# Branch b's last eight outputs through ScalarE, written orders around them, and w_out's first products in two pairs

## The chip, the cores and the metric

The kernel runs on one core of one Trainium2 chip. The metric is the time of one execution in device microseconds (us); a version is told by the median of several executions.

## What is computed

One residual block over a sequence of 1024 positions of width 1024, in float32. Two branches are mixed, gated and projected, and a feed-forward network follows:

```python
def mixer(h, w_in, b_f, conv_w, w_branch, w_out):
    proj = jnp.einsum("bsd,dn->bsn", h, w_in)
    q, k, v, f_logit, g_b, g_c, hc, gate_conv, gate_attn = jnp.split(proj, _SPLITS, axis=-1)
    ya = g_b * causal_depthwise_conv(g_c * hc, conv_w)
    ...
    yb = forgetting_attention(q, k, v, logf)          # 8 heads of 64, 512 wide
    ya_d = jnp.einsum("bsc,cd->bsd", ya, w_branch[0])
    yb_d = jnp.einsum("bsc,cd->bsd", yb, w_branch[1])
    merged = jax.nn.sigmoid(gate_conv) * ya_d + jax.nn.sigmoid(gate_attn) * yb_d
    return jnp.einsum("bsd,de->bse", merged, w_out)
...
x = x + rmsnorm(mixer(rmsnorm(x, ...)), ...)
x = x + rmsnorm(swiglu(rmsnorm(x, ...), w_gate_up, w_down), ...)
```

The lines of this case are the `yb_d` product with its gate and sum (here "branch b") and the first part of the product with `w_out`.

## The kernel before

**How products are formed.** Each float32 operand is cut into a high part (a ScalarE copy into a reduced format, `hi`) and a low part (a VectorE subtraction, `lo`); `split` does both. A product is three matmuls, high by high, high by low, low by high (`mm3`), each of 128 x 128 by 128 x 512. Large products are done by a Strassen scheme of seven block products named by their left operands: A11, A12, A22, S1, S2, S3, S4, with right operands B11, B21, B22, T1 to T4. Left operands of `w_branch` and right operands of `w_out` were prepared earlier and stored (`wb_dram`, `wo_dram`); here they are only loaded.

**Orders.** The framework orders each engine's instructions itself by its own estimate of due times. `strict[0]` names engines whose instructions, from there on, keep the order in which the program text issues them; the wrapper `InOrder` (lines 65 to 80; line 77 issues every instruction, so all profile rows carry L77) marks each such instruction. Instructions issued while their engine is not named may still be moved among the others. Before the change the stretch from line 1546 to 1597 has `("tensor", "sync")`: matmuls and the loads on SyncE's (SP's) queue keep the written order, VectorE and ScalarE do not.

**Branch b (lines 1505 to 1593).** The result `um` has eight tiles d of 128 rows by two halves of columns, n1 and n2. For u = 0 to 3 the scheme gives four outputs, tiles 2u and 2u + 1 in n1 and n2. Eight PSUM banks are held, `pbanks[u]` and `vbanks[u]`. A first loop (1569) does S2, S4, S3 for each u: ScalarE copies the sum in `pbanks[u]` to `u_s[u]`, VectorE adds `vbanks[u]` to it, ScalarE puts the saved product `p_s[u]` back into `vbanks[u]`, and after S3 VectorE adds `pbanks[u]` to `v_s[u]`. `merge` then multiplies an output by its gate and adds it to `um`, two VectorE operations. `u_s` and `v_s` are eight slices of one tile, `temps`, in the place "x2". A second loop (1587) does A22 into `pbanks[u]` and A12 into `vbanks[u]`, in the order `turn_ = (3, 0, 1, 2)`; both are merged by VectorE straight from PSUM.

**Gates.** `gate(d, ns)` (1496) issues a load of a gate tile on SP's queue; the gate of tile 7 was stored before its sigmoid, so for d = 7 it also issues a Sigmoid on ScalarE on what was loaded. Gates of n1 use four `sg` tiles; those of turns u = 2 and 3 are loaded at the end of turns 0 and 1 of the first loop, when a tile comes free. Gates of n2 for u = 3 and 0 use other free tiles; those for u = 1 and 2 follow in `sg`.

**w_out (from 1598).** `um` is cut by rows of the sequence into four pairs of blocks. `first_ops(i)` cuts the first block of pair i into hi and lo, `sums(i)` forms its Strassen sums (on GpSimd for i = 0, on VectorE otherwise). `first(i)` is A11 by B11 into a bank `p1`, copied by ScalarE; `second(i)` is A12 by B21 into a bank `q`, added by VectorE. The loop at 1744 does first(0), first(1), second(0), first(2), second(1), first(3), second(2), second(3). Then `p_s2(0)` is the first product with T2, whose tile `x_tile(2)` has the place "x2"; S1, S3, S4 and A22 follow for each pair, with T1, T3, B22 and T4.

Of the kernel before, what the change touches and what calls it, by code (L numbers as in the profile page):

```python
# [47 lines left out]
def block_kernel(  # L48
# [16 lines left out]
    n1, n2 = slice(0, NC), slice(NC, S)  # L65
    engines = ("tensor", "vector", "scalar", "gpsimd", "sync")
    strict = [()]
# [42 lines left out]
    def add(o, a, b):  # L110
        nc.vector.tensor_tensor(o, a, b, op=ALU.add)
# [4 lines left out]
    def mul(o, a, b):  # L116
        nc.vector.tensor_tensor(o, a, b, op=ALU.mult)
# [11 lines left out]
    def copy(o, a):  # L129
        nc.scalar.activation(o, a, AF.Copy)  # L130

    def split(hi, lo, src):

        copy(hi, src)
        sub(lo, src, f32(hi))
# [399 lines left out]
    def flat(t):  # L535
        return t.rearrange("p a b -> p (a b)")
# [4 lines left out]
    def wtile(tag, bufs, dt=F32, shape=(P, KT, P)):  # L541
        return wpool.tile(list(shape), dt, tag=tag, name=tag, bufs=bufs)

    def raw_t():
        return wtile("raw", 3)

    def hi_t():
        return wtile("hi", 4, F32R)

    def lo_t():  # L550
        return wtile("lo", 3, F32R)

    def s4_t():
        return wtile("s4", 1, F32, (P, 4, P))
# [57 lines left out]
    def bank(psp, name):  # L612
        return psp.tile([P, NC], F32, tag="mm", name=name)

    def prod(ps, w, b, first):
        (ah, al), (bh, bl) = w, b
        kw = {} if first else dict(skip_group_check=True)
        for k in range(4):
            mm3(
                ps,  # L620
                (ah[:, k, :], al[:, k, :]),
                (bh[:, k, :], bl[:, k, :]),
                first and k == 0,
                k == 3,
                **kw,
            )
# [529 lines left out]
    def sg_tile():  # L1156
        return tp_.tile([P, NC], F32, tag="sg", name="sg", bufs=4)
# [281 lines left out]
    def x_tile(n, p=None):  # L1439
        if n == 3:  # L1440
            p, tag = yb_pool, "yb"
        else:
            p, tag = p or wx, f"x{n}"
        return p.tile([P, 2, 4, NC], F32R, tag=tag, name=f"x{n}", bufs=1)
# [6 lines left out]
    def load_wo(o, k):  # L1451
        nc.sync.dma_start(f32(wo[o][:, :, k, :]), wo_dram[o, k])

    PAIRS = ST // 2
    firsts, s3 = [None] * PAIRS, [None] * PAIRS

    def blocks(i):

        a, b = (slice(t * P, (t + 1) * P) for t in (2 * i, 2 * i + 1))
        return um[:, LO, a], um[:, UP, a], um[:, LO, b], um[:, UP, b]  # L1460

    def first_ops(i, th, tl):
        a = slice(2 * i * P, (2 * i + 1) * P)
        if i:
            split(th, tl, um[:, :, a])
            firsts[i] = dict(A11=(th[:, LO], tl[:, LO]), A12=(th[:, UP], tl[:, UP]))
        else:
            firsts[i] = {}
            for o, src, h, l in zip(("A11", "A12"), blocks(i), th, tl):
                split(h, l, src)  # L1470
                firsts[i][o] = h, l

    def kept_halves(t):
        return t[:, n1], t[:, n2]

    def minus(i, o, a, b, op=ALU.subtract):
        e = nc.vector if i else nc.gpsimd
        e.tensor_tensor(o, a, b, op=op)

    def sums(i, t):  # L1480

        a11, a12, a21, a22 = blocks(i)
        s3[i] = t
        minus(i, t, a11, a21)
        minus(i, a21, a21, a22, ALU.add)
        minus(i, a11, a21, a11)
        minus(i, a12, a12, a11)
# [6 lines left out]
    v_s, u_s = ([temps[:, 4 * i + u, :] for u in range(4)] for i in range(2))  # L1494

    def gate(d, ns, sg=None):
        sg = sg_tile() if sg is None else sg
        nc.sync.dma_start(sg, sg_dram[d][1, :, ns])
        if d == KT - 1:
            nc.scalar.activation(sg, sg, AF.Sigmoid)  # L1500
        return sg

    def prod_b(ps, o, u, b, first):
        (wh, wl), (bh, bl) = wb[o], tb[b]
        kw = {} if first else dict(skip_group_check=True)
        for k in range(2):
            m = 4 * k + u
            mm3(
                ps, (wh[:, m, :], wl[:, m, :]), (bh[:, k, :], bl[:, k, :]),
                first and k == 0, k == 1, **kw,  # L1510
            )

    def merge(d, ns, t, c, sg):
        mul(t, c, sg)
        add(um[:, d, ns], um[:, d, ns], t)
# [18 lines left out]
    pbanks = [psm.tile([P, NC], F32, tag="mm", name="pbp") for _ in range(4)]  # L1534
# [23 lines left out]
    vbanks = [psm.tile([P, NC], F32, tag="mm", name="pbv") for _ in range(4)]  # L1558
    for u in range(4):
# [4 lines left out]
    late = [  # L1564
        x for t in (wtile("raw", 3), wtile("sx", 1)) for x in kept_halves(flat(t))
    ]
    turn_ = (3, 0, 1, 2)
    late = [gate(2 * u + 1 - x, n2, late.pop(0)) for u in turn_[:2] for x in range(2)]
    for u in range(4):
        sg2, sg1 = early[2 * u : 2 * u + 2]  # L1570
        prod_b(pbanks[u], S2, u, T2, False)
# [9 lines left out]
            early += [gate(2 * u + 4 + x, n1) for x in range(2)]  # L1581
    first_ops(0, [s4h_t(), s4h_t()], [s4l_t(), s4l_t()])
    sums(0, s4_t())
    late += [gate(2 * u + 1 - x, n2) for u in turn_[2:] for x in range(2)]
    for u in range(4):
        load_wo(B21, u)
    for u in turn_:
        sg1, sg2 = late.pop(0), late.pop(0)
        prod_b(pbanks[u], A22, u, T4, False)
        merge(2 * u + 1, n2, sg1, pbanks[u], sg1)  # L1590
        prod_b(vbanks[u], A12, u, B21, False)
        merge(2 * u, n2, sg2, vbanks[u], sg2)
    for n, o in ((3, T1), (2, T2)):
        wo[o] = x_tile(n)
        for k in range(4):
# [27 lines left out]
    def square(src, acc):  # L1623
        junk = ep.tile([P, NC], F32, tag="junk", name="junk")
        nc.scalar.activation(junk, src, AF.Square, accum_out=acc)

    sx = wtile("sx", 1)
    for i in range(1, PAIRS):
        first_ops(i, hi_t(), lo_t())
        sums(i, ep.tile([P, 4, P], F32, name="s3") if i == 3 else sx[:, 4 * i - 4 : 4 * i])  # L1630

    def load_xt(st):
        xt = ep.tile([P, D], F32, name="xt") if st % 3 == 2 else z_tile("xt")
        nc.gpsimd.dma_start(xt, x2d[st * P : (st + 1) * P, :])
        return xt
# [7 lines left out]
    def first(i):  # L1643
        b1s[i] = pk.tile([P, NC], F32, tag="p1", name="p1")
        prod(b1s[i], firsts[i]["A11"], wob[B11], True)
        t = raw_t() if i < 3 else ep.tile([P, KT, P], F32, name="keep")
        keeps.append(flat(t))
        copy(keeps[i][:, n2], b1s[i])

    def second(i):  # L1650
        q = bank(psm, "q")
        prod(q, firsts[i]["A12"], wob[B21], True)
        add(keeps[i][:, n1], keeps[i][:, n2], q)
        square(keeps[i][:, n1], qas[i][:, 0:1])
# [86 lines left out]
                pinned(turns, "tensor")  # L1741
                ahead(lambda: copy(um[:, 4 * q : 4 * q + 4, ss], tp))

    for step in (0, 1, 2, 3):
        first(step)
        if step:
            second(step - 1)
    second(PAIRS - 1)
    wo[B22] = x_tile(0)
    wob[B22] = both(wo[B22])  # L1750
    for k in range(4):
# [145 lines left out]
    for f in range(NF):  # L1897
# [15 lines left out]
        for g, u, ns in ((g1, u1_, n1), (g2, u2, n2)):  # L1913
            sg = sgs[:, ns]
# [268 lines left out]
```

## Time and profile before

| | |
|---|---|
| median of 3 executions | 1319.69 us (1318.58 to 1319.75) |
| the profiled execution | 1319.07 us, of which the span 1317.3 us |
| granted TensorE clock, mean | 0.999 |
| TensorE busy | 1302.7 us, 99% of the span |
| VectorE busy | 981.4 us, 75% |
| ScalarE busy | 568.4 us, 43% |
| GpSimd busy | 153.6 us, 12% |

Times in rows of the profile are counted from the first instruction of the span; PE is TensorE, DVE VectorE, ACT ScalarE, POOL GpSimd, SPq the queue on which SP issues loads. A row names the tiles as written from read (`temps<-temps,pbp`), then the shapes, a count, and in brackets how long the engine was idle before and what ended that. `pbp` is `pbanks`, `pbv` is `vbanks`, `p` and `q` are the banks of first and second, `x<-wo_dram` are loads of w_out's operands. Branch b's two loops lie at about 564 to 593 us, w_out's eight first products at about 594 to 618 us.

### The profile page before, as it was taken

How to read it: one execution, taken by the hardware profiler on the slowest of the kernel's cores; microseconds unless marked ns; L12 is line 12 of the kernel's file. 1: busy time of each engine (PE TensorE's matmuls, PEld its weight loads, DVE VectorE, ACT ScalarE, POOL GpSimd, SP SyncE). 2: the span in 40 equal slices, each digit the busy share in tenths (PEclk: the TensorE clock that was granted, in tenths of full speed). 3: DMA queues.
4: the chain of work that ended last, by engine and by line, in shares of the span. 5: the costliest groups of instructions: out<-in, count | busy, mean ns of one | idle time of the engine just before them, and what ended most of it. 6: DMA issues, size and time to landing. Idle time of an engine off the chain costs nothing.

```text
span 1317.3 us, 18043 instructions
## 1 busy us (share of the span) xinstructions
PE 1302.7 (99%) x6686; PEld 1084.8 (82%) x6686; DVE 981.4 (75%) x1525; ACT 568.4 (43%) x902; POOL 153.6 (12%) x287
## 2 busy tenths in 40 slices
PE   9999999999999999999999999999999999999997
PEld 8988888888888888877888888888888888888886
DVE  6975978776656877587798789986766776676685
ACT  6642432254455866433676522222232234444452
POOL 0001100021112212020011021211101110000000
PEclk9999999999999999999999999999999999999999
DMA  6347755677846444489266555553323338866541
GB/s 221 110 119 224 196 162 146 168 250 214 240 144 200 162 140 150 154 312 403 81 228 203 160 165 172 184 176 104 104 81 120 105 119 290 311 242 195 156 166 64
DMA packets 207240, 235.13 MB, mean 178 GB/s; under 512 B 12064, under 2 KB 150368, under 8 KB 207152
## 3 DMA queue, kind: packets, MB, share of 16 engines
q1 hardware_dynamic: 159424, 157.13, 38.1%
q0 software_dynamic: 18544, 62.17, 12.8%
q10 hardware_dynamic: 29184, 14.68, 4.5%
q8 instruction: 52, 0.85, 0.3%
q14 instruction: 36, 0.29, 0.1%
HBM read 161.79 MB, written 72.16 MB: 178 GB/s over the span
## 4 chain that ended last, share of the span: by engine, by line
PE 72%; issue 17%; DMA 4%; POOL 2%; DVE 2%; ACT 1%; SPq 0%; POOLq 0%; DVEq 0%; ACTq 0%
PE b L77 37%; PE pd L77 16%; PE pba L77 3%; PE pv L77 3%; PE tps L77 3%; PE po L77 3%; PE p L77 2%; PE sp L77 2%; PE ma L77 1%; PE q L77 1%; PE tp L77 1%; POOL wb_dram L77 1%; DMA x<-wo_dram 1%; DMA raw<-in_w_gate_up_dram 1%; DMA sg<-sg_dram 1%
## 5 line engine op out<-in xcount | busy, mean ns | idle before, releaser
L77 PE MATMUL b<-x,hi 128*128 128x512 f32 x1088 | 335.3, 389 | 0.0
L77 PEld LDWEIGHTS b<-x,hi 128*128 128x128 f32 x1088 | 204.1, 188 | 42.3
L77 PE MATMUL b<-x,lo 128*128 128x512 f32 x544 | 211.7, 389 | 0.0
L77 DVE TENSOR_TENSOR c<-c,b 128x512 f32<-128x512 f32 x193 | 131.3, 681 | 46.4 <-PE b L77 40.1
L77 DVE TENSOR_TENSOR lo<-raw,hi 128x1024 fp32r<-128x1024 f32 x90 | 108.3, 1203 | 71.5 <-PE b L77 61.3
L77 ACT ACTIVATE hi<-raw 128x1024 fp32r<-128x1024 f32 (+1 forms) x96 | 97.4, 1017 | 93.7 <-PE b L77 46.3
L77 PEld LDWEIGHTS b<-x,lo 128*128 128x128 f32 x544 | 102.1, 188 | 21.1
L77 ACT ACTIVATE hi<-sx 128x1024 fp32r<-128x1024 f32 (+1 forms) x42 | 43.7, 1041 | 136.9 <-PE b L77 129.1
L77 ACT ACTIVATE sgf<-c 128x512 f32<-128x512 f32 x31 | 19.6, 633 | 132.3 <-DVE c L77 113.2
L77 DVE TENSOR_TENSOR lo<-sx,hi 128x1024 fp32r<-128x1024 f32 (+1 forms) x42 | 50.3, 1197 | 28.2 <-PE b L77 25.6
L77 DVE TENSOR_TENSOR sx<-raw 128x512 f32<-128x512 f32 x78 | 53.5, 686 | 19.5 <-DMA raw<-in_w_in_dram 9.8
L77 PE MATMUL pd<-hi,lo 128*128 128x512 f32 x160 | 62.3, 389 | 0.0
L77 PE MATMUL pd<-hi 128*128 128x512 f32 x160 | 61.9, 390 | 0.0
L77 PE MATMUL pd<-ghi 128*128 128x512 f32 x148 | 57.6, 389 | 0.0
L77 PE MATMUL pd<-glo,ghi 128*128 128x512 f32 x148 | 57.6, 389 | 0.0
L77 PE MATMUL pd<-ghi,glo 128*128 128x512 f32 x148 | 57.6, 389 | 0.0
L77 PE MATMUL b<-hT34h,hi 128*128 128x512 f32 x136 | 52.9, 389 | 0.0
L77 PE MATMUL b<-hT34l,hi 128*128 128x512 f32 x136 | 52.9, 389 | 0.0
L77 PE MATMUL b<-hT34h,lo 128*128 128x512 f32 x136 | 52.9, 389 | 0.0
L77 PE MATMUL b<-hT12h,hi 128*128 128x512 f32 x136 | 52.9, 389 | 0.0
L77 PE MATMUL b<-hT12l,hi 128*128 128x512 f32 x136 | 52.9, 389 | 0.0
L77 PE MATMUL b<-hT12h,lo 128*128 128x512 f32 x136 | 52.9, 389 | 0.0
(465 smaller groups left out, 3052.7 us busy)
## 6 DMA issues: line engine op xcount, KB each, us to landing
raw<-in_w_gate_up_dram SPq DMA_DIRECT2D x55, 512.0 KB, 3.9
raw<-in_w_in_dram SPq DMA_DIRECT2D x35, 512.0 KB, 5.8
x<-wo_dram SPq DMA_DIRECT2D x28, 512.0 KB, 10.2
a_dramS<-um POOLq DMA_DIRECT2D x44, 256.0 KB, 3.0
a_dramA<-um POOLq DMA_DIRECT2D x33, 256.0 KB, 2.7
wo_dram<-h ACTq DMA_DIRECT2D x16, 448.0 KB, 4.3
wo_dram<-l ACTq DMA_DIRECT2D x16, 448.0 KB, 4.7
sg<-sg_dram SPq DMA_DIRECT2D x28, 256.0 KB, 3.0
```

Of the source, the lines that this page charges most:

```text
L77: ins = getattr(self.engine, name)(*args, **kw)
```

## The change

- The first loop, the second loop and what is between them are issued with `("tensor", "sync", "vector", "scalar")`: VectorE's and ScalarE's instructions there keep the written order too. After the second loop only SP's does, as far as the loads of T1 and T2.
- The second loop runs u = 0, 1, 2, 3. Its eight outputs are copied by ScalarE from PSUM into `v_s[u]` and `u_s[u]`, and the merges read those.
- `first_ops(1)` is issued ahead of the second loop. `first_ops(2)` and `(3)`, then `sums(1)` to `(3)`, are issued behind it with VectorE's order written.
- w_out's first products run first(0), first(1), second(0), second(1), first(2), first(3), second(2), second(3).

```diff
-    turn_ = (3, 0, 1, 2)
-    late = [gate(2 * u + 1 - x, n2, late.pop(0)) for u in turn_[:2] for x in range(2)]
+    late = {u: [gate(2 * u + 1 - x, n2, late.pop(0)) for x in range(2)] for u in (3, 0)}
+    strict[0] = ("tensor", "sync", "vector", "scalar")
     for u in range(4):
         sg2, sg1 = early[2 * u : 2 * u + 2]
         prod_b(pbanks[u], S2, u, T2, False)
         copy(u_s[u], pbanks[u])
         prod_b(vbanks[u], S4, u, B22, False)
         add(u_s[u], u_s[u], vbanks[u])
         copy(vbanks[u], p_s[u])
         merge(2 * u, n1, u_s[u], u_s[u], sg2)
         prod_b(pbanks[u], S3, u, T3, False)
         add(v_s[u], v_s[u], pbanks[u])
         merge(2 * u + 1, n1, v_s[u], v_s[u], sg1)
         if u < 2:
             early += [gate(2 * u + 4 + x, n1) for x in range(2)]
     first_ops(0, [s4h_t(), s4h_t()], [s4l_t(), s4l_t()])
     sums(0, s4_t())
-    late += [gate(2 * u + 1 - x, n2) for u in turn_[2:] for x in range(2)]
+    first_ops(1, hi_t(), lo_t())
+    late |= {u: [gate(2 * u + 1 - x, n2) for x in range(2)] for u in (1, 2)}
     for u in range(4):
         load_wo(B21, u)
-    for u in turn_:
-        sg1, sg2 = late.pop(0), late.pop(0)
+    for u in range(4):
         prod_b(pbanks[u], A22, u, T4, False)
-        merge(2 * u + 1, n2, sg1, pbanks[u], sg1)
+        copy(v_s[u], pbanks[u])
         prod_b(vbanks[u], A12, u, B21, False)
-        merge(2 * u, n2, sg2, vbanks[u], sg2)
+        copy(u_s[u], vbanks[u])
+        for x, t in enumerate((v_s[u], u_s[u])):
+            sg = late[u][x]
+            merge(2 * u + 1 - x, n2, sg, t, sg)
+    strict[0] = ("sync",)
     for n, o in ((3, T1), (2, T2)):
...
     sx = wtile("sx", 1)
+    strict[0] = ("vector",)
+    for i in range(2, PAIRS):
+        first_ops(i, hi_t(), lo_t())
     for i in range(1, PAIRS):
-        first_ops(i, hi_t(), lo_t())
         sums(i, ep.tile([P, 4, P], F32, name="s3") if i == 3 else sx[:, 4 * i - 4 : 4 * i])
+    strict[0] = ()
...
-    for step in (0, 1, 2, 3):
-        first(step)
-        if step:
-            second(step - 1)
-    second(PAIRS - 1)
+    for step in (first, second):
+        step(0)
+        step(1)
+    for step in (first, second):
+        step(2)
+        step(3)
```

## The prediction

> **What bounds the kernel now.** I read the page first (its span and busy times), then the list of who waited for whom on TensorE alone around the changed lines, then the timeline of each engine there.
>
> ```profile
> span 1317.3 us, 18043 instructions
> PE 1302.7 (99%) x6686; PEld 1084.8 (82%) x6686; DVE 981.4 (75%) x1525; ACT 568.4 (43%) x902; POOL 153.6 (12%) x287
> ```
>
> TensorE is busy 99% of the span, so a microsecond matters only if TensorE stands still in it. The list of waits on TensorE from 540 to 700 us has four entries; these three lie in the lines that are changed.
>
> ```profile
> PE p L77 <- DVE lo L77: 1.3, 1, 1.3
> PE p L77 <- DVE sg L77: 1.2, 1, 1.2
> PE pbp L77 <- DVE temps L77: 1.2, 1, 1.2
> ```
>
> The timeline of TensorE shows them one by one. A row is start, length, tiles, count, and in brackets the idle time before it.
>
> ```profile
> 575.02 0.39 PE L77 MATMUL pbp<-yh,hi 128*128 128x512 f32 x1
> 576.38 0.39 PE L77 MATMUL pbp<-yh,hi 128*128 128x512 f32 x1
> 579.29 0.50 PE L77 MATMUL pbp<-yh,hi 128*128 128x512 f32 x1
> 580.56 0.39 PE L77 MATMUL pbp<-yh,lo 128*128 128x512 f32 x1
> 582.11 0.50 PE L77 MATMUL pbp<-yh,hi 128*128 128x512 f32 x1 [1.16 <-DVE temps L77]
> 591.78 0.39 PE L77 MATMUL pbv<-b,raw 128*128 128x512 f32 x1
> 594.53 0.73 PE L77 MATMUL p<-x,s4h 128*128 128x512 f32 x2 [1.22 <-DVE sg L77]
> 597.38 0.61 PE L77 MATMUL p<-x,hi 128*128 128x512 f32 x2
> 599.26 0.50 PE L77 MATMUL p<-x,lo 128*128 128x512 f32 x1 [1.26 <-DVE lo L77]
> 617.98 0.39 PE L77 MATMUL p<-x,hi 128*128 128x512 f32 x1
> ```
>
> 575.02 is the S3 product of u = 2 in branch b's first loop; 576.38 is the next product, six matmuls later, so a matmul takes 1.36/6 = 0.2267 us when nothing is late. 617.98 is the first T2 product of w_out (p_s2(0)). Between these two rows stand 168 matmuls: 6 + 18 in the rest of the first loop, 48 in the second loop, 96 in w_out's eight first products. They need 168 x 0.2267 = 38.08 us and take 42.96: this stretch loses 4.88 us. Its pieces: S3 of u = 3 starts 0.19 late at 579.29; the second loop's first product 1.32 late (580.79 to 582.11); first(0) 1.39 late (593.14 to 594.53); first(1) stands 1.42 (597.84 to 599.26); each restart's first matmul is 0.11 longer (0.50 against 0.39).
>
> **The change, part by part.**
>
> *The second loop from u = 0 (turn_ goes).* Today it starts with u = 3, whose bank pbanks[3] has only just been filled, and VectorE empties it late:
>
> ```profile
> 580.77 0.69 DVE L77 TENSOR_TENSOR temps<-temps,sg 128x512 f32<-128x512 f32 x1 [0.71 <-DMA sg<-sg_dram]
> 581.38 0.68 DVE L77 TENSOR_TENSOR temps<-temps,pbp 128x512 f32<-128x512 f32 x1
> 593.80 0.67 DVE L77 TENSOR_TENSOR sg<-pbv,sg 128x512 f32<-128x512 f32 x1
> 598.00 1.21 DVE L77 TENSOR_TENSOR lo<-um,hi 128x1024 fp32r<-128x1024 f32 x1
> ```
>
> From u = 0 the bank was read three turns earlier. The 1.32 + 0.11 goes.
>
> *Eight outputs by ScalarE.* Each bank is copied (0.58 to 0.60 us a copy, rows below) every 1.36 us, so ScalarE keeps up, and a bank is free about 0.65 us after its product instead of after VectorE's queue (593.80 above is the read that held first(0) until 594.53). The 1.39 + 0.11 goes. VectorE still does 16 operations there, now from SBUF; no row shows one shorter than the 0.61 us between 580.77 and 581.38, so I count no gain.
>
> *first_ops(1) ahead of the second loop.* Its lo part is the operation at 598.00 that first(1) waits for. It moves ahead of the second loop's merges; 1.42 + 0.11 goes.
>
> So far everything that was lost goes, 4.88. What is added is a wait.
>
> *The written order on ScalarE.* From the first loop on, ScalarE too keeps the order of the text. At the end of turn u = 1 the text loads gates 6 and 7, and gate(7, n1) puts a Sigmoid on ScalarE that must wait for its load. In the text it stands before both copies of u = 2. Today it runs behind all of them:
>
> ```profile
> 571.93 0.60 ACT L77 ACTIVATE pbv<-p_s 128x512 f32<-128x512 f32 x1 [1.55 <-DVE temps L77]
> 573.86 0.60 ACT L77 ACTIVATE temps<-pbp 128x512 f32<-128x512 f32 x1 [1.32 <-PE pbp L77]
> 578.12 0.63 ACT L77 ACTIVATE raw<-raw 128x512 f32<-128x512 f32 x1 [1.51 <-DMA raw<-sg_dram]
> 578.66 0.58 ACT L77 ACTIVATE temps<-pbp 128x512 f32<-128x512 f32 x1
> 582.70 0.63 ACT L77 ACTIVATE sg<-sg 128x512 f32<-128x512 f32 x1 [2.00 <-DMA sg<-sg_dram]
> ```
>
> ```profile
> 577.53 0.32 SPq L77 DMA_DIRECT2D sg<-sg_dram  x1
> sg<-sg_dram SPq DMA_DIRECT2D x1, 256.0 KB, 5.1
> ```
>
> 573.86 is the copy of u_s[2], 582.70 the Sigmoid; its load is issued at 577.53 and lands 5.1 us later, at 582.6. The diff touches no load ahead of it and SP's order was written already, so it lands then again. ScalarE, after the copy at 571.93, now stands at the Sigmoid (the one at 578.12, gate 7 of n2, is outside the written order and fits into that wait). Behind it on ScalarE: copy(u_s[2]). That copy must empty pbanks[2] before TensorE's S3 of u = 2 may write there, and VectorE's add of u = 2 needs it too. So: Sigmoid at 582.70; next operation 0.54 later (578.12 to 578.66); copy 0.58, done at 583.82; TensorE 0.05 later (579.24 to 579.29), at 583.87 instead of 575.02. **TensorE stands for 8.85 us**, and the restart costs 0.11.
>
> *The rate after such a stand.* No row of this stretch shows so long a wait (the longest is 1.42), so I bound the restart. Lower end: full rate at once, 0. Upper end: the only start from rest in this trace, the kernel's first transposes:
>
> ```profile
> 1.47 4.32 PE L77 MATMUL spin<-ident 128*128 128x128 f32 x19 [1.47 <-POOL ident masks.py:199]
> 6.57 1.04 PE L77 MATMUL spin<-ident 128*128 128x128 f32 x8
> ```
>
> Nineteen start about 0.22 us apart (less the last one's length, some 0.4, over 18 steps); the same instruction from 6.57 on runs 0.11 apart. TensorE thus ran at half rate for 4.3 us although the clock column says 1.00, and lost 2.1 us. A stand of 8.85 is nearer to that start than to a stall of 1.4, so I take 2.1 and keep 0 as the other end. [...]
>
> *VectorE's written order in w_out, the pairs.* After its last merge VectorE has lo of blocks 2 and 3 ahead of twelve sums. Restarted as above, the second loop's products would end at about 602.2, and first(2) comes four products of 2.72 later, at 613. VectorE's merges end at 606 to 608: sixteen operations at 0.61 behind lo(1), which waits for the last n1 merge at about 594; two may be slowed while GpSimd forms block 0's sums, as today:
>
> ```profile
> 587.99 1.19 DVE L77 TENSOR_TENSOR s4l<-um,s4h 128x512 fp32r<-128x512 f32 x1
> 589.10 1.77 DVE L77 TENSOR_TENSOR um<-um,raw 128x512 f32<-128x512 f32 x1
> ```
>
> hi and lo of block 2 add 1.06 + 1.2, so 611 at the latest: 2 us of cover. The pairs change the order of products only. Price 0.
>
> *T2's load.* The copies use temps, whose place x_tile(2) takes for T2; its four loads now wait until the last merge, about 607, and hold SP's queue.
>
> ```profile
> 586.07 12.95 SPq L77 DMA_DIRECT2D x<-wo_dram  x12
> 601.36 9.86 SPq L77 DMA_DIRECT2D x<-wo_dram  x8
> 613.27 4.34 SPq L77 DMA_DIRECT2D x<-wo_dram  x4
> ```
>
> A load takes 12.95/12 = 1.1 us of the queue: T2 is there by about 615, needed at 624 (602.2 + eight products). Behind it follow the eight of T3 and T4, two rows of gains and the four of B22: fourteen loads, to about 631, B22 being needed at 635. Price 0, with 4 us of cover; if that is gone, each late load costs 1.1.
>
> *Downstream.* From 602 to 653 TensorE has no idle time that could absorb a shift:
>
> ```profile
> 602.00:653.00 51.00, 51.00 (x227) 42.23 (x226) 32.44 (x58) 24.66 (x50) 2.15 (x4) 1.00 0.55 211
> ```
>
> **The sum.** Added 8.85 + 0.11 + 2.1 = 11.06, removed 4.88: 6.2 us longer. The profiled execution took 1319.07 us in all (1.8 around its span), 0.6 below the median of 1319.69, so 1325.3 by its own time or 1325.9 by the median; I say 1325.6.
>
> **The rivals.** *A, faster:* the Sigmoid does not hold the copies back, because its place stays behind them or its load is early. Then only the removals count, less 0.3 for a copy that is just late as at 579.29: 4.6 off, 1315. For it: today's order. Against it: the wrapper keeps every ScalarE instruction written under the new tuple, and this one is. It decides where the Sigmoid's load lands before about 578.6, since a stand that costs 4.9 cancels the removals; today it lands 4 us after that. *B, no half rate:* the same stand and full rate behind it: 6.2 - 2.1 = 4.1, 1323.5. For it: the clock column's 1.00 at the start. *C, w_out is late as well:* VectorE's lo of block 2 or B22's load outlasts its cover by 1 to 2 us: 1327.5. Against it: the 2 and 4 us above. *D:* the wait is there but shorter, some load landing early, and it cancels the removals: 1319.7.
>
> **How the numbers follow.** Forecast 0.60, B 0.14, C 0.08, A 0.13, D 0.05. The range leaves out A and D: 1321 (B with a load 2.5 us earlier) to 1328.8 (C with a longer slow stretch). A difference of 0.2%, 2.6 us, is what a measurement of this kernel can tell: faster 0.13, same 0.07 (D and B's low end), slower 0.80.
>
> **What will show it.** Right: on ScalarE, a wait of some 10 us for the load of sg between a copy into pbv and a copy from pbp; on TensorE one wait of nearly 9 us at the S3 product of u = 2, put down to ScalarE; matmuls some 0.45 apart (twice 0.2267) for some 4 us behind it; and no wait at the second loop's first product, at first(0) or at first(1). Wrong: the Sigmoid behind the copies as today; or its load issued before 574; or a wait at first(2) or p_s4(0), which would put the loss into w_out.

## The result and the profile after

| | before | after |
|---|---|---|
| median of 4 executions | 1319.36 us (1318.58 to 1319.75) | 1334.46 us (1333.10 to 1335.45) |
| ratio of the times | | 1.0115 (95%: 1.0097 to 1.0132) |
| the profiled execution, and its span | 1319.07, 1317.3 us | 1333.1, 1331.3 us |

The change costs 15.1 us by the medians and 14.0 between the two profiled executions. The sign was forecast; the time lies 5.7 us above the range that was given.

From the page of after (busy times, then a line of the slices with the granted TensorE clock in tenths):

```profile
span 1331.3 us, 18049 instructions
PE 1305.8 (98%) x6686; PEld 1087.1 (82%) x6686; DVE 984.7 (74%) x1525; ACT 572.4 (43%) x910; POOL 153.9 (12%) x287
PEclk9999999999999999979999999999999999999999
```

TensorE has the same 6686 matmuls and is 3.1 us longer busy in a span that is 14.0 longer; one slice of forty, around 566 to 599 us, shows a lower clock, a 7 among the 9s. The list of waits on TensorE from 540 to 720 us has two entries (total, times, longest):

```profile
PE pbp L77 <- ACT temps L77: 14.5, 2, 11.0
PE tp L77 <- ACT um L77: 0.7, 1, 0.7
```

The three waits of before are gone, and two others stand in their place, both for ScalarE, both at an S3 product. One was forecast, two came. TensorE's timeline:

```profile
566.80 0.39 PE L77 MATMUL pbv<-yh,lo 128*128 128x512 f32 x1
578.21 0.80 PE L77 MATMUL pbp<-yh,hi 128*128 128x512 f32 x1 [11.02 <-ACT temps L77]
578.80 0.63 PE L77 MATMUL pbp<-yl,hi 128*128 128x512 f32 x1
...
582.64 0.41 PE L77 MATMUL pbp<-yl,hi 128*128 128x512 f32 x1
...
588.37 0.39 PE L77 MATMUL pbv<-yh,lo 128*128 128x512 f32 x1
592.20 0.50 PE L77 MATMUL pbp<-yh,hi 128*128 128x512 f32 x1 [3.44 <-ACT temps L77]
...
593.08 0.63 PE L77 MATMUL pbp<-yh,hi 128*128 128x512 f32 x1
593.50 0.63 PE L77 MATMUL pbp<-yl,hi 128*128 128x512 f32 x1
...
632.20 0.62 PE L77 MATMUL p<-x,hi 128*128 128x512 f32 x2
```

The first stand, 566.80 to 578.21, is at S3 of **u = 0**; less the 0.227 of a matmul it loses 11.18. Behind it the starts are 0.43 apart up to 582.64: another 2.2 with the restart. The second, 588.37 to 592.20, is at S3 of u = 2 and loses 3.60; from 593.08 to 596.06 the starts are 0.43 apart again, 1.7 with the restart. These four make 18.7. From the first loop's first product (564.30) to p_s2(0) (632.20) after takes 67.90 us; before took 53.84 (564.14 to 617.98), of which 4.88 were its three waits. 18.7 - 4.88 = 13.8 of the 14.06 between them.

ScalarE's timeline says what the two stands wait for:

```profile
564.50 0.60 ACT L77 ACTIVATE temps<-pbv 128x512 f32<-128x512 f32 x1 [0.52 <-PE pbv L77]
577.04 0.63 ACT L77 ACTIVATE raw<-raw 128x512 f32<-128x512 f32 x1 [11.94 <-DMA raw<-sg_dram]
577.57 0.58 ACT L77 ACTIVATE temps<-pbp 128x512 f32<-128x512 f32 x1
...
585.50 0.60 ACT L77 ACTIVATE pbv<-p_s 128x512 f32<-128x512 f32 x1 [1.58 <-DVE temps L77]
591.03 0.63 ACT L77 ACTIVATE sg<-sg 128x512 f32<-128x512 f32 x1 [4.93 <-DMA sg<-sg_dram]
591.57 0.58 ACT L77 ACTIVATE temps<-pbp 128x512 f32<-128x512 f32 x1
```

The row at 577.04 is the Sigmoid of gate 7 of **n2** (`raw<-raw`). Before, it ran behind six of the first loop's copies, at 578.12. Now it is ahead of the first of them, copy(u_s[0]), and stands 11.94 us for its load. The brackets of the old row, 1.51 us for the same load, already told when that load lands; behind the copies the wait did no harm. The row at 591.03 is the Sigmoid of gate 7 of n1, between copy(vbanks[1], p_s[1]) and copy(u_s[2]), as forecast, but with a later load. SP's queue, and the VectorE operation that frees the gate tile for that load:

```profile
566.08 1.55 SPq L77 DMA_DIRECT2D raw<-sg_dram  x2
...
588.27 0.32 SPq L77 DMA_DIRECT2D sg<-sg_dram  x1
```

```profile
587.55 0.69 DVE L77 TENSOR_TENSOR temps<-temps,sg 128x512 f32<-128x512 f32 x1
```

n2's load is issued at 566.08 and lands at about 577. n1's is issued when the multiply that starts at 587.55 ends, at 588.27 instead of 577.53 before, because VectorE stood behind the first stand too.

### The profile page after: what moved, and what is told of

It is laid out like the page before. It is cut to its first block, busy times and chain, and to the rows that moved or that the text cites. A ratio compares the mean times of both kernels' runs of the same rounds, so it can differ in the third digit from the quotient of the medians.

```text
span 1331.3 us, 18049 instructions
## 1 busy us (share of the span) xinstructions
PE 1305.8 (98%) x6686; PEld 1087.1 (82%) x6686; DVE 984.7 (74%) x1525; ACT 572.4 (43%) x910; POOL 153.9 (12%) x287
## 4 chain that ended last, share of the span: by engine, by line
PE 73%; issue 17%; DMA 3%; POOL 2%; DVE 2%; ACT 1%; SPq 0%; DVEq 0%; POOLq 0%; ACTq 0%
PE b L77 36%; PE pd L77 16%; PE pba L77 3%; PE pv L77 3%; PE tps L77 3%; PE po L77 3%; PE p L77 2%; PE sp L77 2%; PE pbp L77 2%; PE ma L77 1%; DMA raw<-sg_dram 1%; PE q L77 1%; PE tp L77 1%; POOL wb_dram L77 1%; DMA wb_dram<-bl 1%
## 5 line engine op out<-in xcount | busy, mean ns | idle before, releaser
L77 DVE TENSOR_TENSOR sx<-raw 128x512 f32<-128x512 f32 x78 | 53.6, 687 | 19.7 <-DMA raw<-in_w_in_dram 10.7
```

The lines of the kernel that those rows point to most:

```text
L77: ins = getattr(self.engine, name)(*args, **kw)
```

## The experiments

Each was timed beside the kernel before; the first four share one chip (before: 1318.30 us) and so do the last four (before: 1318.50). Executions of one kernel differ by 1 to 5 us, so the profiled execution of each is also read by place: from the first loop's first product to w_out's first S1 product (below, "the changed lines"), and from there to the end of the span. Both are from TensorE's timelines, in us:

| | before | after | e1 | e2 | e3 | e4 | e5 | e6 | e7 | e8 |
|---|---|---|---|---|---|---|---|---|---|---|
| changed lines | 56.56 | 70.62 | 56.80 | 61.65 | 66.09 | 57.88 | 68.47 | 52.08 | 52.26 | 55.85 |
| behind them | 696.6 | 696.4 | 696.9 | 696.5 | 696.6 | 700.6 | 697.0 | 696.8 | 698.0 | 696.7 |

The theory at the start: both Sigmoids stand at the head of ScalarE, n2's because it is issued ahead of the written stretch, and the stand and the half rate behind it make the loss. The rival causes are the rest of the written orders, the eight copies and w_out's new order.

**e1_both_moved.** Both Sigmoids leave `gate`; n1's is issued in the first loop's last turn, behind ScalarE's two copies of that turn, n2's ahead of the second loop.

```diff
-        if d == KT - 1:
-            nc.scalar.activation(sg, sg, AF.Sigmoid)
...
+        if u == 3:
+            nc.scalar.activation(sg1, sg1, AF.Sigmoid)
...
+    nc.scalar.activation(late[3][0], late[3][0], AF.Sigmoid)
```

> Both Sigmoids of gate 7 are issued where their loads have long landed (n1: in turn u = 3 of the first loop, n2: ahead of the second loop); all else as changed. Theory 1 (two Sigmoids at the head of ScalarE cost two stands of 11.2 and 3.6 us and the half rate behind them, some 3.7 us): no wait on ScalarE in the first loop, 4.9 us off the kernel before, less up to 3 us if VectorE's merges now make first(2) late: 1314.5 to 1318. Theory 2 (VectorE's written order is what frees banks and gate tiles late): still above 1328. Theory 3 (the eight copies or T2's late load cost the time): still above 1328, with the wait in w_out.

Measured: 1320.04 us, ratio 1.0007 (0.9998 to 1.0016). That is 1.7 us above before, where the change was 15.1 above: 13.4 come back, and no wait is left in branch b. The interval does not tell e1 from before, and in the traces the changed lines are 0.2 longer; 2 to 5.5 us of what was expected are missing. TensorE now waits in w_out, at first(2). The rows are from the waits on TensorE, TensorE's timeline, VectorE's, GpSimd's, and the windows (length, then busy us of PE, PEld, DVE, ACT and POOL, granted clock, DMA share, GB/s):

```profile
PE p L77 <- ACT hi L77: 2.4, 1, 2.4
...
PE p L77 <- DVE lo L77: 0.5, 1, 0.5
```

```profile
605.61 0.74 PE L77 MATMUL p<-x,hi 128*128 128x512 f32 x2 [2.44 <-ACT hi L77]
606.87 0.54 PE L77 MATMUL p<-x,lo 128*128 128x512 f32 x1 [0.52 <-DVE lo L77]
```

```profile
587.64 2.39 DVE L77 TENSOR_TENSOR s4l<-um,s4h 128x512 fp32r<-128x512 f32 x2
589.96 2.30 DVE L77 TENSOR_TENSOR lo<-um,hi 128x1024 fp32r<-128x1024 f32 x1
592.18 1.78 DVE L77 TENSOR_TENSOR sx<-temps,sx 128x512 f32<-128x512 f32 x1
```

```profile
587.87 5.55 POOL L77 TENSOR_TENSOR um<-um 128x512 f32<-128x512 f32 x3 [10.22 <-DVE um L77]
```

```profile
605.61:610.62 5.01, 4.49 (x12) 3.24 (x13) 5.01 (x7) 4.22 (x8) 0.00 (x0) 0.66 0.98 344
```

hi and lo of block 2 come after VectorE's last merge, and first(2) is 2.60 + 0.69 late; then the clock is 0.66 in the mean over 5 us, a further 1.6. That is the place of the prediction's rival C. VectorE is held up while GpSimd forms block 0's sums beside it: the three rows above are long, which e6 tests.

**e2_n2_moved.** Only n2's Sigmoid is moved; n1's stays where the change has it. This is the kernel that the prediction described.

```diff
-        if d == KT - 1:
+        if d == KT - 1 and ns == n1:
...
+    nc.scalar.activation(late[3][0], late[3][0], AF.Sigmoid)
```

> Only the Sigmoid of gate 7 of n2 is moved behind its load; that of n1 stays at the end of turn u = 1. Theory 1: the first stand at u = 0 is gone and the one at u = 2 is as long as the prediction had it, 8.9 us, with half rate behind it: 1325 to 1327. If the stand at u = 2 is only the 3.6 us of the changed kernel: 1319 to 1321. Theories 2 and 3: near 1334.

Measured: 1324.90 us, ratio 1.005 (1.0037 to 1.0063), 0.1 us under the range expected. Waits on TensorE, ScalarE's timeline, TensorE's:

```profile
PE pbp L77 <- ACT temps L77: 7.5, 1, 7.5
```

```profile
571.92 0.60 ACT L77 ACTIVATE pbv<-p_s 128x512 f32<-128x512 f32 x1 [1.58 <-DVE temps L77]
581.47 0.63 ACT L77 ACTIVATE sg<-sg 128x512 f32<-128x512 f32 x1 [8.94 <-DMA sg<-sg_dram]
```

```profile
582.64 0.80 PE L77 MATMUL pbp<-yh,hi 128*128 128x512 f32 x1 [7.49 <-ACT temps L77]
```

One stand, at S3 of u = 2, 7.65 us lost, and 2.1 behind it at half rate. The forecast's mechanism is that of this kernel. That its time (1325.6) is too is partly chance: the stand is 1.2 shorter than forecast, and the changed lines are 5.1 longer than before's where the medians are 6.6 apart and the forecast said 6.2.

**e3_n1_moved.** The reverse: n1's Sigmoid is moved, n2's stays.

```diff
-        if d == KT - 1:
+        if d == KT - 1 and ns == n2:
...
+        if u == 3:
+            nc.scalar.activation(sg1, sg1, AF.Sigmoid)
```

> Only the Sigmoid of gate 7 of n1 is moved (to turn u = 3); that of n2 stays ahead of the first loop. Theory 1: the stand of 11.2 us at u = 0 and 2.1 us of half rate stay, the one at u = 2 goes: 1319.4 + 11.2 + 2.1 - 4.9 = 1327.8, up to 1330 if VectorE makes first(2) late. Theories 2 and 3: near 1334.

Measured: 1329.50 us, ratio 1.0081 (1.0068 to 1.0095). Waits on TensorE and ScalarE's timeline:

```profile
PE pbp L77 <- ACT temps L77: 10.9, 1, 10.9
...
```

```profile
577.03 0.63 ACT L77 ACTIVATE raw<-raw 128x512 f32<-128x512 f32 x1 [11.80 <-DMA raw<-sg_dram]
```

The stand at u = 0 is there by itself, 11.04 lost, with half rate behind it (starts 0.43 apart from 578.79 to 583.05, 2.4 us lost with the restart). Over e1, n1's Sigmoid alone costs 4.9 us (e2), n2's alone 9.5 (e3), both 13.4 (15.1 less 1.7). In the changed lines the same differences are 4.9, 9.3 and 13.8. These are not the sizes of the stands: e1 loses in w_out what e2 and after do not, and with both Sigmoids in place the second stand is 3.60 instead of 7.65.

**e4_no_scalar.** The Sigmoids stay; ScalarE's order isn't written.

```diff
-    strict[0] = ("tensor", "sync", "vector", "scalar")
+    strict[0] = ("tensor", "sync", "vector")
```

> As changed, but ScalarE's order is not written; VectorE's is. Theory 1: both Sigmoids go behind the copies again and no stand remains: 1314.5 to 1318. Theory 2 (VectorE's written order): 1328 to 1334.

Measured: 1323.75 us, ratio 1.0036 (1.0022 to 1.005): 6 to 9 us more than expected. Waits on TensorE, ScalarE's timeline, then a row of TensorE's and a window further on:

```profile
PE p L77 <- ACT hi L77: 4.1, 1, 4.1
PE tp L77 <- ACT um L77: 2.0, 1, 2.0
PE tp L77 <- DVE raw L77: 1.3, 2, 1.2
```

```profile
577.95 0.63 ACT L77 ACTIVATE raw<-raw 128x512 f32<-128x512 f32 x1 [1.39 <-DMA raw<-sg_dram]
...
605.52 1.99 ACT L77 ACTIVATE hi<-um 128x1024 fp32r<-128x1024 f32 x2
```

```profile
675.19 1.11 PE L77 MATMUL tp<-ident,tt 128*128 128x128 f32 x4 [2.03 <-ACT um L77]
```

```profile
660.00:680.00 20.00, 16.74 (x75) 13.40 (x74) 16.70 (x28) 12.87 (x25) 2.69 (x5) 0.91 0.62 214
```

The theory's own part holds: by this one word n2's Sigmoid goes back behind the copies (577.95; before 578.12) and branch b has no stand. The time was missed in two places. first(2) is 4.22 late, with half rate behind it, some 2.0 us by an estimate (57.88 less 4.22, less the 51.68 that before's changed lines take without their 4.88); that lies in the changed lines, which take 1.3 us more than in before and 1.1 more than in e1. Some 4 us are lost behind them, where neither the change nor this edit has a line: transposes wait 1.19 at 671.40 and 2.03 at 675.19, and the clock from 660 to 680 is 0.91 (in e1 one wait of 1.39 there, and 1.00). So most of the 3.7 us between e4 and e1 is not the worth of ScalarE's written order in the changed lines; the later work ran in another order, and why it came out slower isn't settled. Why first(2) is later than in e1 is only partly seen: hi starts 1.0 later (605.52 against 604.50) and TensorE is there 0.6 earlier.

**e5_filler.** The change, with TensorE kept busy in most of both stands: matmuls of a zero weight (44 at u = 0, 14 at u = 2) onto `vbanks[3]`, to which they add nothing.

```diff
+    def fillers(n):
+        for _ in range(n):
+            nc.tensor.matmul(
+                vbanks[3], zero, tb[T2][0][:, 0, :], start=False, stop=False,
...
+        fillers({0: 44, 2: 14}.get(u, 0))
         prod_b(pbanks[u], S3, u, T3, False)
```

> The changed kernel with TensorE kept busy through both stands: 44 matmuls behind S4 of u = 0 and 14 behind S4 of u = 2, with a zero left operand, added onto vbanks[3] (they add 0). They fill 10.0 of 11.2 us and 3.2 of 3.6 us. Theory 1 (it is TensorE's standing idle that halves its rate afterwards): matmuls 0.23 apart behind both stands, and 2.3 + 1.6 us less than the changed kernel's 1334.4: about 1330.5. Rival (the slow matmuls come from something else at that time, loads or ScalarE's and VectorE's use of PSUM): still 0.43 apart, 1334 or more.

Measured: 1330.26 us, ratio 1.0087 (1.0073 to 1.0101). TensorE's timeline:

```profile
567.14 10.13 PE L77 MATMUL pbv<-yh,zero 128*128 128x512 f32 x44
579.75 0.50 PE L77 MATMUL pbp<-yh,hi 128*128 128x512 f32 x1 [2.47 <-ACT temps L77]
580.09 0.40 PE L77 MATMUL pbp<-yl,hi 128*128 128x512 f32 x1
580.33 0.40 PE L77 MATMUL pbp<-yh,lo 128*128 128x512 f32 x1
```

S3 comes no earlier for it (ScalarE's copy releases it at about 579.7, in after at 578.2), but the starts behind it are 0.24 apart and not 0.43, and so are those behind the second stand, from 591.71 on; the granted clock is 1.00 in both places. So the 2.2 + 1.7 that the rows of after lost with the restarts are all but gone. In this execution the first stand is 1.4 longer than in after, which leaves the changed lines 2.15 shorter. By the medians the filler is worth 3.3 us (the differences to before on each chip, 11.8 against 15.1) or 4.2 (the two directly). The half rate was the price of TensorE's idle time, not of what the matmuls read.

**e6_sums_dve.** e1, and block 0's sums on VectorE, issued behind first_ops(3), instead of on GpSimd ahead of the second loop.

```diff
-        e = nc.vector if i else nc.gpsimd
-        e.tensor_tensor(o, a, b, op=op)
+        nc.vector.tensor_tensor(o, a, b, op=op)
...
-    sums(0, s4_t())
+    s3_0 = s4_t()
...
+    sums(0, s3_0)
```

> e1 with block pair 0's four sums on VectorE behind lo(3) instead of on GpSimd beside the merges. Theory 1 (in e1 TensorE waits at first(2), 2.6 us, because VectorE's merges and lo(2) come late, three of its operations being slowed by GpSimd by some 2.7 us in all): first(2) not or hardly late, no half rate behind it, 4 us less than e1's 1320.0: about 1316. Rival (GpSimd does not slow VectorE on this path): as e1 or up to 2.4 us later for the four added operations: 1320 to 1322.

Measured: **1315.24 us, ratio 0.9975 (0.9966 to 0.9984)**, faster than both kernels. Waits on TensorE from 540 to 720 us (all of them) and VectorE's timeline:

```profile
PE tp L77 <- ACT um L77: 1.4, 1, 1.4
```

```profile
586.75 1.48 DVE L77 TENSOR_TENSOR s4l<-um,s4h 128x512 fp32r<-128x512 f32 x2
588.48 1.23 DVE L77 TENSOR_TENSOR lo<-um,hi 128x1024 fp32r<-128x1024 f32 x1 [0.26 <-ACT hi L77]
589.62 0.68 DVE L77 TENSOR_TENSOR sx<-temps,sx 128x512 f32<-128x512 f32 x1
```

The same three rows take 3.39 us; beside GpSimd they took 6.47. With those 3.1 us VectorE is in time: first(2) is 0.25 late instead of 3.3, there is no half rate (the mean clock is 0.999, in e1 0.997), and branch b with w_out's first products loses next to nothing: the changed lines are 4.5 us shorter than before's and 4.7 shorter than e1's. The edit changes the engine and the place of the sums at once; sums on GpSimd behind the merges were not tried.

**e7_sums_inter.** e6, and each turn's two merges as two multiplies, then two adds, so that no add follows the multiply it needs.

```diff
-            sg = late[u][x]
-            merge(2 * u + 1 - x, n2, sg, t, sg)
+            mul(late[u][x], t, late[u][x])
+        for x in range(2):
+            d = 2 * u + 1 - x
+            add(um[:, d, n2], um[:, d, n2], late[u][x])
```

> e6 with the second loop's merges written as two products, then two additions, so that no operation reads what the one ahead of it wrote (0.61 instead of 0.72 us to the next operation: eight times 0.11, 0.9 us earlier). Theory 1: what is left of the wait at first(2) goes; 1315, all of the 4.9 us of the three old waits gained. Rival: nothing is left to gain, as e6.

Measured: 1316.76 us, ratio 0.9984 (0.9975 to 0.9993): not 1315, and behind e6. The eight merges do take less (9.7 us against 10.7 in e6), but the changed lines take as long as in e6: nothing was left to gain there, as the rival had it. TensorE now waits behind them:

```profile
PE b L77 <- DVE lo L77: 1.3, 1, 1.3
```

That is in w_out's S1, 1.48 lost; the order of VectorE's later work, which the framework chooses, has changed with it. It isn't settled further.

**e8_no_copies.** e7 without ScalarE's eight copies: VectorE's multiplies read PSUM.

```diff
-        copy(v_s[u], pbanks[u])
...
-        copy(u_s[u], vbanks[u])
-        for x, t in enumerate((v_s[u], u_s[u])):
+        for x, t in enumerate((pbanks[u], vbanks[u])):
```

> e7 without ScalarE's eight copies: the merges read PSUM. Theory 1: VectorE, which reaches the second loop's merges only behind lo(1), some 8 us after that loop began, now holds the banks: first(0) or a product of the second loop is 4 to 5 us late, with half rate behind it, 1320 to 1322. Rival (the copies gain nothing, the bank of first(0) comes free in time): as e7.

Measured: 1318.27 us, ratio 0.9994 (0.9985 to 1.0003): slower than e7, as expected, by 1.5 instead of 3 to 5. Waits on TensorE, its timeline, VectorE's:

```profile
PE p L77 <- issue: 2.4, 1, 2.4
```

```profile
594.18 1.19 PE L77 MATMUL p<-x,s4h 128*128 128x512 f32 x2 [2.43 <-issue]
```

```profile
593.40 0.68 DVE L77 TENSOR_TENSOR sg<-pbv,sg 128x512 f32<-128x512 f32 x1
```

first(0) is 2.59 late, with 1.5 of half rate behind it. In the changed lines that is 3.6 more than e7; the medians are closer because e7 loses 1.5 behind them, which e8 does not. The profile names no releaser; VectorE's read of a bank that first(0) takes ends at 594.08, 0.1 before it starts, as 593.80 did before the change. The copies do what the change has them for.

## Why the prediction was wrong, point by point

- **The step that failed** is the half sentence in brackets, "the one at 578.12, gate 7 of n2, is outside the written order and fits into that wait". It took the Sigmoid's place from the old profile. The instruction is issued ahead of the stretch, and with ScalarE's order written it ran ahead of the stretch's ScalarE work (after, e3); without, behind the copies of three turns (e4, by one word). It cost a stand of 11.18 us and 2.2 of half rate that were not in the sum, and none of the three signs of being wrong named it. That any unmarked instruction issued earlier keeps its place ahead of marked ones is the obvious reading, but only this one was tried.
- **The stand that was forecast** is right in place and cause, and mis-sized: 8.85 forecast; 7.65 where it is alone (e2, its Sigmoid at 581.47, where 582.70 was taken from before); 3.60 in after. "The diff touches no load ahead of it" held, but the load of n1's gate can't be issued before VectorE frees a tile; in after that decides (588.27), because VectorE was held by the first stand.
- **The half rate** (2.1 taken, 0 kept as the other end): 2.2 and 1.7 in after, 2.1 in e2, and it goes when TensorE is kept busy (e5, starts 0.24 apart). Rival B is out; there the clock column shows it (0.50 from 578.21 to 582.64), which it did not at the kernel's start (1.00). The range's upper end, 1328.8, puts 1.3 us on rival C's 1327.5 for a longer slow stretch; no run shows that term: the tails lost 1.5 to 2.4 us.
- **The 4.88 that goes:** all three waits are gone, and e8 shows first(0)'s come back without the copies.
- **w_out and VectorE's order, price 0 with 2 us of cover:** right in after (first(2) is a restart's 0.11 late) and in e2, but the 2 us of cover were not there: in e2 lo of block 2, started at 611.16, lets first(2) go on at 612.44, also a restart's 0.11 late. Part of the cover was the stand itself. In e1 it was gone and 3.3 + 1.6 came back: two terms were too small, the merges at 1.33 each (0.72 and 0.61 between starts, where 2 x 0.61 was taken) and the operations beside GpSimd (3.1 longer in all). Rival C was no rival of the forecast but what stands next when the forecast's stand is taken away.
- **T2's load, price 0:** right; p_s2(0) has no wait at 632.20.
- **Rival A** needed the Sigmoid out of ScalarE's way. e1 is its case, and its 1315 was not reached there, for the reason just given; e6 is its time, with the sums moved too. **Rival D**, a shorter stand because a load lands early, did not come: after's second stand is shorter though its load is issued 10.7 us later than before, because TensorE came there late as well.

## What to carry to other kernels

- Before an engine's order is written down, list what that engine was given before the stretch and inside it that waits for a load, and put each one's issue place, not its time in the old profile, against the landing. One such instruction at the head of an engine that empties PSUM cost 11 us of TensorE here.
- The stands of TensorE here, 2.4 to 11.2 us, cost their length and, in all but one of the cases above (2.47 us in e5), a tail at half rate (1.5 to 2.4 us); and once a stand is gone, the cover that it gave to every other engine is gone too, so the next wait must be counted without it.

## What the runs showed of the hardware

**The half rate behind a wait.** The windows of after, over the first stand, the matmuls behind it, and the matmuls behind the second:

```profile
566.80:578.21 11.41, 0.39 (x3) 0.01 (x1) 0.02 (x1) 1.11 (x2) 0.00 (x0) 0.75 0.97 382
578.21:582.64 4.43, 4.43 (x11) 3.50 (x12) 3.45 (x6) 0.60 (x1) 0.00 (x0) 0.50 0.19 62
...
592.20:596.42 4.22, 4.22 (x12) 3.31 (x13) 3.81 (x6) 0.60 (x1) 0.00 (x0) 0.60 0.19 62
```

The starts are 0.43 apart where the clock is 0.50 (578.21 to 582.64), and 0.23 apart where it is 1.00 (583 to 588). An estimate from these windows, with the clock taken as either 1 or 0.5 throughout: a mean of 0.60 over 4.22 us is 3.38 us at half. The first stand gives 0.5 x 11.41 + 4.43 = 10.1, three times as much; e1's window above 0.68 x 5.01 = 3.41. The stand need not be long: 2.44 us of idle time did it in e1, 1.6 us after the restart, and 2.43 in e8; in e4 it was 2.03, with 1.19 some 3 us ahead of it. 2.47 in e5 did not, nor did any of before's 1.16 to 1.26. So a wait of 2.4 to 2.5 us cost another 1.6 us in e1, 1.5 in e8 and nothing in e5; what decides between them is not shown.

**GpSimd beside VectorE.** Beside three sums on GpSimd three groups of VectorE (four operations) took 0.91, 1.07 and 1.10 us longer (e1 against e6). Having GpSimd form block 0's sums beside the merges cost the kernel 5.0 us here (e1 is 1.7 above before, e6 3.3 below; 4.7 in the changed lines), because VectorE was what w_out waited for.
